# Layer 1's gate products moved from the third query chunk to the attention's last units

## The chip, the cores and the metric

One Trainium2 chip, one core of it. The metric is the device time of one execution in microseconds (us); of several executions the median is given. A core has five engines with a queue each: PE (matrix products and transposes), DVE (vector), ACT (activations, copies), POOL (general), and SP, which here only issues transfers (DMA). Each takes its instructions in the order in which they stand; an instruction whose operand is not ready holds up everything behind it on the same engine.

## The reference

The kernel computes one inference step of a trunk with two layers on 128 context tokens and 512 latent tokens, width 1024. Layer 0 is gated grouped-query attention (16 query heads, 4 key/value heads of width 64), layer 1 a gated linear recurrence in two directions. Both are modulated by vectors that come from a conditioning vector `c` (latent tokens) or `c_ctx` (context tokens):

```
def _adaln(cond, w, b):
    mod = jax.nn.silu(cond) @ w + b
    return jnp.split(mod, 3, axis=-1)          # shift, scale, gate

for i in range(2):
    sh_p, sc_p, g_p = _adaln(c_ctx, ada_w[i], ada_b[i])
    sh_s, sc_s, g_s = _adaln(c, ada_w[i], ada_b[i])
    hp = xp * (1.0 + sc_p) + sh_p
    hs = xs * (1.0 + sc_s) + sh_s
    out_p, out_s = mixer_i(hp, hs)             # i = 0: attention, i = 1: recurrence
    xp = _layer_norm(ALPHA * xp + g_p * out_p, ln_gain[i], ln_bias[i])
    xs = _layer_norm(ALPHA * xs + g_s * out_s, ln_gain[i], ln_bias[i])
```

The gate of layer 1 (`g_p`, `g_s` with i = 1) depends only on the conditioning vectors and on a 1024 x 1024 block of `ada_w[1]`. It is used first where layer 1 closes, at the very end of the program.

## The kernel before

All tokens (five tiles of 128) stay on the core. The program runs in two halves; the first (keys, values, queries and attention of layer 0) is recorded in program order, and a scheduler that works with its own model of time then decides how the instructions of each engine follow one another. Tuned tables in the source set what the program order is.

Attention is cut in units. A unit is one query head with 256 latent tokens (`sample_unit`) or four heads with the context tokens (`prompt_unit`). A sample unit has two *fronts*, of 128 queries each: scores on PE (`sc`, lines 923 and 924), the row maximum on DVE (`nm`, line 1018), the exponential on ACT (`p`, line 1023), the reciprocal of the sum on DVE (`rc`, line 1028), and the scaling of the probabilities on POOL (line 1029). Its *back* is ten transposes on PE (`pt`, line 1036), copied out of PSUM by ACT or DVE (`pts`, line 928). Two heads together then have their products with the values on PE (`pot`, line 950), and DVE multiplies them into the gate path `gs` (line 955). Scores have two buffers in PSUM, `pot` one. Fronts run two units ahead of backs.

`att_gen` yields after every such piece, and `weave(att, side, SIDE_AT)` runs `SIDE_AT[n]` steps of side work after the n-th piece. Side work is a list that is taken from its head: the query projections of chunks 1 to 3 (`q1`, `q2`, `q3`: products `qmm`, lines 389 to 391, and their norm and rotation), then `w` (the first four pieces of the attention's output weights split into a high part by ACT, `wohi`, line 262, and a low part by DVE, `wolo`, line 264), then `s` (splits of `gs`). What is called the third query chunk is `q2`, since the first is chunk 0.

Each query chunk takes a generator as *filling* (`q_gen`, table `FILL_AT`): chunk 1 the gate products of layer 0, chunk 2 those of layer 1 (`ada_gen`), chunk 3 five column jobs (`cols_gen`: ten DVE instructions, `spill`, line 361). `ada_gen(layer)` loads the bias to `acc`, and four times takes two pieces of `ada_w` (512 KB each), multiplies them with the conditioning vectors (`ada_mms`, line 312: four products of 32 x 256 for each piece, in four column strips) and adds the sum to `acc` on DVE (line 349); at its end POOL issues four small transfers of `acc` to `gated` in DRAM (line 353). The first layer's gate is read back from there by `gate_load` (line 341) inside the last chunk's filling, the second's in the recurrence's tail.

Weights come through one ring of three 512 KB buffers (`raw`, line 241) in the order of the list `order`, issued by SP. `pump` keeps two pieces taken ahead; a piece's transfer starts when the piece three before it has been used up. So the list's order, and the engine that uses a piece, set when the next ones arrive.

Of the kernel before, what the change touches and what calls it, by code (L numbers as in the profile page):

```python
# [34 lines left out]
HALVES = ((0, 320), (320, 640))  # L35
HALF_PIECES = (slice(0, 512), slice(512, 1024))
RAW_AHEAD = 2
FILL_AT = {1: '0b0e2e', 2: '0b0e2e4e', 3: '0a0b0e2e4e'}
LEAD = (1, 1)
RAW_START = 8  # L40
EARLY = 2
# [2 lines left out]
D_OUTS = 1  # L44
SIDE_T = 2.2
SIDE_AT = (
    "0100021120010100020100012001210201010101000002111001021000000130"
    "2002020010001200011201020101300010100102000000201112120001100001"
    "3100002000111000000310010102010113001000012000120300210000012")
RES_AT = 6  # L50
SEVEN = range(1, RH - 1)
FORMS_AT = 3
# [12 lines left out]
COLS = [(s, ft) for s in range(2) for ft in range(KT)]  # L65
COLS_LATE = 5
# [88 lines left out]
def hybrid_step(ctx: ExitStack, tc: tile.TileContext, a: dict, o: dict):  # L155
# [16 lines left out]
    def bank1(name):  # L172
        if "b1" not in pools:
            return bank2(name)[:, 0, :]
        return pools["b1"].tile([P, 512], F32, tag="b1", name=name)
# [40 lines left out]
    order = deque()  # L216
    pin, pass_on = tc.keep_in_program_order, lambda ins: ins

    def pump(most=RAW_AHEAD):
        while order:  # L220
            start = order[0] in FIRST
            if len(ahead) >= (RAW_START if start else most):
                break
            src = order.popleft()
            if src[0] == "x":
                c = slice(src[1] * CW, (src[1] + 1) * CW)
                pin(nc.sync.dma_start(xt[:, :TS, c], a["xs"][:, c].rearrange("(t p) d -> p t d", p=P)))
                pin(nc.sync.dma_start(xt[:, TS, c], a["xp"][:, c]))
                continue
            if src[0] == "rope":  # L230
                rope_loads()
                continue
            if src[0] == "sil":
                for s in range(2):
                    pin(nc.sync.dma_start(silb[:, s, :], a["cond_r"][s:s + 1, :].to_broadcast((P, D))))
                continue
            raw = (raw0 if start else rawp).tile([P, 1024], F32, tag="raw", name="raw")
            if src[0] == "kvh":
                pin(nc.sync.dma_start(raw[:, :512], piece(src)))
            else:  # L240
                (pass_on if src[0][:3] == "rec" else pin)(nc.sync.dma_start(raw, piece(src)))
            ahead.append((src, raw))
# [56 lines left out]
    def take(src):  # L299
        pump()  # L300
        got, raw = ahead.popleft()
        assert got == src, (got, src)
        return raw
# [3 lines left out]
    def ada_mms(ps, sup, i):  # L307

        for k in (2 * i, 2 * i + 1):
            raw = take(("ada_s", sup, k))  # L310
            for q in range(4):
                nc.tensor.matmul(ps[32 * q:32 * q + 32, :CW], sil[:, k, :], raw[:, q * CW:(q + 1) * CW],
                                 start=(k % 2 == 0), stop=(k % 2 == 1))
            pump()
# [24 lines left out]
    def gate_load(layer, eng):  # L339
        for s in range(2):  # L340
            eng.dma_start(gate[layer][:, s, :], gated[layer][s:s + 1, :].to_broadcast((P, D)))

    def ada_gen(layer):
        acc = rowp.tile([P, CW], F32, tag="row", name="acc")
        nc.gpsimd.dma_start(acc, a["ada_bias"][layer])
        for i in range(4):
            ps = bank1("adaps")
            ada_mms(ps, layer, i)
            nc.vector.tensor_tensor(acc, acc, ps[:, :CW], ALU.add)
            yield  # L350
        yield
        for q in range(4):
            nc.gpsimd.dma_start(gated[layer][:, q * CW:(q + 1) * CW], acc[32 * q:32 * q + 2, :])
        yield

    def ada_cols(job, raw, spill, after):

        s, ft = job
        for c in range(2):
            with tc.issue_after(after()) if after else ExitStack():  # L360
                nc.vector.scalar_tensor_tensor(spill(), raw, 1.0, silb[:, c, :], ALU.mult, ALU.mult,
                                               accum_out=shsc[1][:, s, ft, c:c + 1])
            yield
        if ft == KT - 1:
            nc.vector.tensor_tensor(shsc[1][:, s], shsc[1][:, s], view(adab, (3 + s) * KT, [[1, KT], [0, 2]]), ALU.add)
# [4 lines left out]
    def cols_gen():  # L370
        for job in COLS[len(COLS) - COLS_LATE:]:
            yield from ada_cols(job, take(("ada_c",) + job), spare, None)
            pump()
        gate[0] = gsp.tile([P, 2, D], F32, tag="gate", name="gate0")
        gate_load(0, nc.gpsimd)
# [29 lines left out]
    def pieces(name, c, n=2):  # L405
        return [(name, c, i) for i in range(n)]

    PIECES = [(nh, i) for nh in range(2) for i in range(4)]
    OUT1 = [(nh, i) for i in range(4) for nh in range(2)]
    def ada_pieces(sup):  # L410
        return [("ada_s", sup, k) for k in range(KT)]
# [16 lines left out]
        order.extend(pieces("attn_w_in", c))  # L428
    for c in range(3):
        order.extend(pieces("attn_w_in", c + 1))  # L430
        order.extend(ada_pieces(c) if c < 2 else [("ada_c",) + job for job in COLS[len(COLS) - COLS_LATE:]])
    order.extend(("attn_w_out", nh, i) for nh, i in PIECES)
    order.extend(("rec_w_in", h, i) for h in range(RH) for i in range(5))
    order.extend(("rec_w_out", nh, i) for nh, i in OUT1)

# [200 lines left out]
    def rms_stat(ps, n):  # L636
        ss = tiny.tile([P, 8], F32, tag="ss", name="ss")
        squares(ps, n, ss[:, :4 * n])
        rstd = tiny.tile([P, 8], F32, tag="rstd", name="rstd")
        rsqrt(rstd[:, :4 * n], ss[:, :4 * n], 1.0 / HD, NORM_EPS)  # L640
        return rstd
# [29 lines left out]
    def rms_scale(r, n, rstd):  # L671
        qn = prep.tile([P, 2 * CW], F32, tag="qn", name="qn")
        nc.vector.tensor_tensor(view(qn, 0, [[HD, 4 * n], [1, HD]]), view(r, 0, [[HD, 4 * n], [1, HD]]),
                                view(rstd, 0, [[1, 4 * n], [0, HD]]), ALU.mult)
        return qn
# [63 lines left out]
    def tok_unit(w, tt0, n, name):  # L739
        ps = bank1(name)  # L740
        for i in range(n):
            yield from tok_gen(ps[:, i * CW:(i + 1) * CW], w, tt0 + i, hhi, hlo)
        return ps

    def q_gen(c, X, fill):

        w = Weights("attn_w_in", c, (nc.vector, nc.vector), tuple(last_split))
        yield
        spots = {FILL_AT[c][i:i + 2] for i in range(0, len(FILL_AT[c]), 2)}
        pend = None  # L750
        for tt0, n in UNITS:
            ps = None
            gen = tok_unit(w, tt0, n, "qmm")
            step = 0
            while ps is None:
                try:
                    next(gen)
                except StopIteration as e:
                    ps = e.value
                    break  # L760
                step += 1
                yield
                if f"{tt0}{'0abcd'[step]}" in spots:
                    next(fill, None)
                    yield
            rstd = rms_stat(ps, n)
            r = rope_raw(ps, tt0, n, cosq, sinq, qg)
            yield
            if pend:
                for i in range(pend[1]):  # L770
                    pend[0](i)
                    yield
            if f"{tt0}e" in spots:
                next(fill, None)
                yield
            yield
            qn = rms_scale(r, n, rstd)
            yield
            pend = (q_split(qn, tt0, n, c % 2, X, bank1), n)
        yield  # L780
        for _ in fill:
            yield
        for i in range(pend[1]):
            pend[0](i)
            yield

    xq = [rpool("xq0", 1)]
    Xs = {0: xq[0].tile([P, 4, NT], F32R, tag="X", name="X0")}
# [218 lines left out]
    back_of = [0]  # L1007
# [97 lines left out]
    side = Side()  # L1105
# [57 lines left out]
    def split_gs(ks):  # L1163
        for k in ks:
            split_act(hhi[:, k, :], hlo[:, k, :], gs[:, k, :], nc.gpsimd if k < 6 else nc.vector)
            yield
# [4 lines left out]
    def prefetch_gen():  # L1171
        wb.close()
        pq.close()
        woa.append(ws.enter_context(pool("woa", 1)))
        yield from wo_gen(0, PIECES[:4], woa[0])

    def q_next(c):
        Xs[c] = xq[c % 2].tile([P, 4, NT], F32R, tag="X", name=f"X{c}")
        yield from q_gen(c, Xs[c], ada_gen(c - 1) if c < 3 else cols_gen())

    for c in range(1, 4):
        side.items.append((f"q{c}", q_next(c), lambda c=c: front_of[0] >= c - 1))
    side.items += [("w", prefetch_gen()), ("s", split_gs(range(6)), lambda: back_of[0] == 3)]
    for _ in range(3):
        side.step()
    with tc.issue_after(last_qmm[0]):
# [705 lines left out]
    side = token_forms()  # L1892
    for h in range(RH):
        H = {} if h else H
        if h == RH - 1:
            sxs.close()
            side = reload_gen()
# [203 lines left out]
```

## Time and profile before

| | us |
|---|---|
| median of 3 runs | 820.88 |
| lowest, highest | 820.34, 822.41 |
| the profiled execution, its time | 820.92 |
| its span | 819.2 |

The span is the time from the first to the last instruction that the profiler recorded; 1.7 us of the time lie around it. In the profile PE is a busy matrix engine, PEld its weight loads. A row of a view by stretches gives start:end, the length, and for PE, PEld, DVE, ACT and POOL the busy time with the number of instructions; the last three are the granted clock of PE, the DMA engines' busy share, and GB/s. In the profiled execution the query chunks and the attention's units lie at 134 to 325 us; the products of layer 1's gate at 193 to 229 us; the last product of the last query chunk at 269.1 us; the column jobs at 234 to 288 us; the first four output-weight splits at 291 to 301 us; the first product of the output projection at 325.0 us.

### The profile page before, as it was taken

What the parts mean: (1) busy time and instruction counts of PE and PEld (TensorE: products, weight loads), DVE (VectorE), ACT (ScalarE), POOL (GpSimd) and SP (SyncE); (2) the same over time, 40 slices, a digit from 0 to 9 for tenths busy, and PEclk for the clock granted to TensorE, in tenths of its full rate; (3) what the DMA queues carried; (4) which work ended last, traced back from release to release, by engine and by line L of the source; (5) the groups of instructions that cost most, each with busy time, mean ns of one, the idle gap of its engine ahead of it and who ended that gap; (6) DMA issues with size and microseconds to landing.
All of it is one profiled execution on the core that took longest, in us unless ns stands there. A gap on an engine that the chain in (4) does not pass through costs nothing.

```text
span 819.2 us, 19274 instructions
## 1 busy us (share of the span) xinstructions
PE 792.4 (97%) x7953; PEld 700.9 (86%) x7953; DVE 598.3 (73%) x1083; ACT 447.0 (55%) x890; POOL 215.1 (26%) x261
## 2 busy tenths in 40 slices
PE   8999999999999989999999999999999999999994
PEld 6789999878888766888899999998999999897874
DVE  4567767686678885676799787868787876788376
ACT  2252545566566786132565666757484855766242
POOL 0124001353434843011500224122240404131121
PEclk9999999999999999999999999999999999999998
DMA  9944344234130150621431342324242344232341
GB/s 327 395 158 157 104 155 134 100 110 150 52 129 28 36 197 18 240 103 50 141 104 54 100 118 76 104 69 125 64 134 72 103 102 162 70 110 74 136 153 77
DMA packets 36630, 98.12 MB, mean 120 GB/s; under 512 B 5296, under 2 KB 12480, under 8 KB 36544
## 3 DMA queue, kind: packets, MB, share of 16 engines
q1 hardware_dynamic: 25872, 78.95, 28.7%
q0 software_dynamic: 4768, 14.18, 5.8%
q10 hardware_dynamic: 5904, 3.78, 1.6%
q8 instruction: 62, 1.02, 0.5%
q14 instruction: 24, 0.20, 0.1%
HBM read 86.06 MB, written 10.83 MB: 118 GB/s over the span
## 4 chain that ended last, share of the span: by engine, by line
PE 80%; DVE 8%; DMA 4%; ACT 3%; issue 2%; POOL 2%; SPq 0%; DVEq 0%; ACTq 0%; POOLq 0%
PE vgps L1383 8%; PE vgps L1379 4%; PE outp L1213 4%; PE outp L1215 4%; PE outp L1214 4%; PE rps L1451 4%; PE pot L950 3%; PE rps L1405 3%; PE rps L1407 3%; PE rps L1406 3%; PE pt L1036 3%; PE rps L1453 3%; PE rps L1452 3%; PE acc L568 3%; PE lv L1682 2%
## 5 line engine op out<-in xcount | busy, mean ns | idle before, releaser
L1029 POOL TENSOR_SCALAR p<-p,rc 128x640 f32<-128x640 f32 x64 | 56.9, 894 | 115.5 <-DVE rc L1028 98.3
L1720 POOL COPY At<-near 32x160 f32<-32x160 f32 x32 | 15.0, 469 | 191.8 <-PE lv L1688 173.7
L1023 ACT ACTIVATE p<-sc,nm 128x640 f32<-128x640 f32 x64 | 51.1, 801 | 25.2 <-DVE nm L1018 15.5
L1018 DVE TENSOR_REDUCE nm<-sc 128x1 f32<-128x640 f32 x64 | 51.7, 816 | 12.7 <-PE sc L924 12.6
L1405 PE MATMUL rps<-h1hi,rw 128*128 128x320 f32 x176 | 55.4, 315 | 0.0
L1407 PE MATMUL rps<-h1hi,rw 128*128 128x320 f32 x176 | 54.5, 310 | 0.1
L1406 PE MATMUL rps<-h1lo,rw 128*128 128x320 f32 x176 | 54.5, 309 | 0.0
L1036 PE MATMUL pt<-small,p 128*128 128x128 f32 x320 | 49.0, 277 | 3.0 <-DVE pts L928 1.2
L1383 PE MATMUL vgps<-rw,h1hi 128*128 128x512 f32 x180 | 48.3, 392 | 0.0
L1655 ACT COPY kc<-A 128x640 f32<-128x640 f32 x47 | 37.5, 798 | 18.5 <-DVE A L1706 12.5
L1036 PEld LDWEIGHTS pt<-small,p 128*128 128x128 f32 x320 | 36.5, 140 | 12.0 <-issue 5.6
L928 ACT COPY pts<-pt 128x512 f32<-128x512 f32 x64 | 36.1, 589 | 14.8 <-PE pt L1036 14.6
L923 PE MATMUL sc<-kk,X 128*128 128x320 f32 x128 | 42.4, 340 | 1.8 <-ACT p L1023 1.6
L1726 ACT COPY At<-lv 32x160 f32<-32x160 f32 (+1 forms) x48 | 15.8, 329 | 49.6 <-PE lv L1688 49.2
L950 PE MATMUL pot<-pts,vv 128*64 128x256 f32 x320 | 38.3, 384 | 2.1 <-DVE pts L928 2.0
L380 PE MATMUL gps<-hhi,whi 128*128 128x320 f32 x128 | 40.0, 312 | 0.1
L381 PE MATMUL gps<-hlo,whi 128*128 128x320 f32 x128 | 39.6, 309 | 0.0
L382 PE MATMUL gps<-hhi,wlo 128*128 128x320 f32 x128 | 39.5, 309 | 0.0
L1383 PEld LDWEIGHTS vgps<-rw,h1hi 128*128 128x128 f32 x180 | 33.1, 188 | 6.6
L924 PE MATMUL sc<-klo,X 128*128 128x320 f32 x128 | 38.6, 310 | 0.0
L1383 PE MATMUL vgps<-wspare,h1hi 128*128 128x512 f32 x140 | 38.1, 394 | 0.0
L389 PE MATMUL qmm<-whi,hhi 128*128 128x256 f32 x120 | 35.0, 292 | 0.1
(347 smaller groups left out, 2623.2 us busy)
## 6 DMA issues: line engine op xcount, KB each, us to landing
raw<-in_rec_w_in SPq DMA_DIRECT2D x40, 512.0 KB, 3.8
raw<-in_ada_m SPq DMA_DIRECT2D x16, 512.0 KB, 8.3
raw<-in_attn_w_in SPq DMA_DIRECT2D x16, 512.0 KB, 4.6
raw<-in_ada_s SPq DMA_DIRECT2D x16, 512.0 KB, 3.7
adaraw<-in_ada_c SPq DMA_DIRECT2D x11, 512.0 KB, 5.4
raw<-in_attn_w_out SPq DMA_DIRECT2D x8, 512.0 KB, 4.1
raw<-in_rec_w_out SPq DMA_DIRECT2D x8, 512.0 KB, 3.6
raw<-in_ada_c SPq DMA_DIRECT2D x5, 512.0 KB, 4.4
```

The source lines that it names most:

```text
L380: nc.tensor.matmul(ps[:, :320], w.hi(k)[:, c], hhi[:, k, t], start=(k == 0), stop=False)
L381: nc.tensor.matmul(ps[:, :320], w.hi(k)[:, c], hlo[:, k, t], start=False, stop=False)
L923: nc.tensor.matmul(out, X[:, h, t0:t0 + P], kk[:, c, k0:k1], start=True, stop=False)
L950: nc.tensor.matmul(pot[j * HD:(j + 1) * HD, :CW], vv[:, slot, c * HD:(c + 1) * HD], moving[j], start=first, stop=last)
L1018: nc.vector.tensor_reduce(nm[:, 0:1], sc[:, :, :320], AX.XY, ALU.max, negate=True)
L1023: return nc.scalar.activation(halves(p[:]), sc[:, :, :320], AF.Exp, bias=nm[:, 0:1], accum_out=su[:, 0:1])
L1029: nc.gpsimd.tensor_scalar(p, p, rs[:, 0:1], 1.0, ALU.mult, ALU.mult)
L1036: nc.tensor.transpose(pt[:, i * 256 + q * P:i * 256 + (q + 1) * P], ps[q][:, (k0 + i) * P:(k0 + i + 1) * P], ident)
L1383: nc.tensor.matmul(out, h1hi[:, k, t], wvg[i][:, k % 4].rearrange("p e n -> p (e n)"), start=(k == 0), stop=(k == KT - 1))
L1405: nc.tensor.matmul(ps[:, j, :320], hi[:, k, :], h1hi[:, k, t], start=(k == 0), stop=False)
L1406: nc.tensor.matmul(ps[:, j, :320], hi[:, k, :], h1lo[:, k, t], start=False, stop=False)
L1407: nc.tensor.matmul(ps[:, j, :320], lo[:, k, :], h1hi[:, k, t], start=False, stop=(k == KT - 1))
```

## The change

The gate products of layer 1 leave the filling of chunk 2 (its entry in `FILL_AT` is empty, and its generator too) and become an item of their own, `g`, in the side list, behind `w` and ahead of `s`. In the order of weight pieces their eight pieces move from behind chunk 2's weights to a place behind the first four pieces of the output weights. `SIDE_AT` loses the steps that the filling took and has its last third laid out anew.

```diff
-FILL_AT = {1: '0b0e2e', 2: '0b0e2e4e', 3: '0a0b0e2e4e'}
+FILL_AT = {1: '0b0e2e', 2: '', 3: '0a0b0e2e4e'}
 SIDE_AT = (
-    "0100021120010100020100012001210201010101000002111001021000000130"
-    "2002020010001200011201020101300010100102000000201112120001100001"
-    "3100002000111000000310010102010113001000012000120300210000012")
+    "0100021120010100020100012001210201010101000001110001021000000130"
+    "1002020010001100011101020101300010100102000000201112120001100001"
+    "3100002000100001001001001201111010100000000000000000000000000")
...
         order.extend(pieces("attn_w_in", c + 1))
-        order.extend(ada_pieces(c) if c < 2 else [("ada_c",) + job for job in COLS[len(COLS) - COLS_LATE:]])
-    order.extend(("attn_w_out", nh, i) for nh, i in PIECES)
+        order.extend(((lambda: ada_pieces(0)), list, lambda: [("ada_c",) + job for job in COLS[len(COLS) - COLS_LATE:]])[c]())
+    order.extend(("attn_w_out", nh, i) for nh, i in PIECES[:4])
+    order.extend(ada_pieces(1))
+    order.extend(("attn_w_out", nh, i) for nh, i in PIECES[4:])
...
-        yield from q_gen(c, Xs[c], ada_gen(c - 1) if c < 3 else cols_gen())
+        yield from q_gen(c, Xs[c], (ada_gen(0), iter(()), cols_gen())[c - 1])
...
-    side.items += [("w", prefetch_gen()), ("s", split_gs(range(6)), lambda: back_of[0] == 3)]
+    side.items += [("w", prefetch_gen()), ("g", ada_gen(1)), ("s", split_gs(range(6)), lambda: back_of[0] == 3)]
```

What the scheduler makes of it differs in many small places between the second query chunk and the attention's end; no instruction is added or taken away. Lines behind the edits are two higher in the changed kernel (312, 349 and 353 stay; `sc` is 925 and 926, `pt` 1038, `pot` 952).

SP's queue, before: the transfers of weight pieces from chunk 2's weights on (`ada_s` are gate pieces, `ada_c` the column jobs').

```order
L241 DMA raw<-in_attn_w_in 128x1024 x2
L241 DMA raw<-in_ada_s 128x1024 x8
L241 DMA raw<-in_attn_w_in 128x1024 x2
L241 DMA raw<-in_ada_c 128x1024 x5
L241 DMA raw<-in_attn_w_out 128x1024 x8
```

And in the changed kernel, the same place:

```order
L241 DMA raw<-in_attn_w_in 128x1024 x4
L241 DMA raw<-in_ada_c 128x1024 x5
L241 DMA raw<-in_attn_w_out 128x1024 x4
L241 DMA raw<-in_ada_s 128x1024 x8
L241 DMA raw<-in_attn_w_out 128x1024 x4
```

The eight gate pieces moved past chunk 3's weights, the column jobs and four output pieces; the last four output pieces come behind them.

PE's queue, before: where the last two pieces' products of a gate step stood, among scores and transposes of the second chunk's units, ahead of chunk 3's projection.

```order
L924 MATMUL sc<-klo,X_1580 128x320
L734 MATMUL qps<-identr,qs_2473 128x128 x4
L312 MATMUL adaps<-raw,sil 32x256 x8
L1036 MATMUL pt<-small,p 128x128 x6
L923 MATMUL sc<-kk,X_1580 128x320
```

In the changed kernel the first five pieces' products stand here, behind a product with the values (`pscp` are the scores of the last context unit; the rows of its four heads, and of the second half of a front, are alike and left out):

```order
L952 MATMUL pot<-pts,vv 64x256 x10
L312 MATMUL adaps<-raw,sil 32x256 x4
L1038 MATMUL pt<-small,p 128x128 x4
L312 MATMUL adaps<-raw,sil 32x256 x4
L1038 MATMUL pt<-small,p 128x128 x4
L925 MATMUL sc<-kk,X_2863 128x320
...
L926 MATMUL pscp<-klo,X_2863 128x128
L312 MATMUL adaps<-raw,sil 32x256 x4
L1038 MATMUL pt<-small,p 128x128 x2
L312 MATMUL adaps<-raw,sil 32x256 x8
L1038 MATMUL pt<-small,p 128x128 x4
```

All 32 products of layer 1's gate moved from the second chunk's units to the last units, and stand close together there.

DVE's queue in the changed kernel, at the fourth and last of the early output-weight splits:

```order
L264 TENSOR_TENSOR wolo<-raw,wohi 128x1024
L1020 TENSOR_REDUCE nm<-sc 128x1
L1030 RECIPROCAL rc<-su 128x1 x2
L957 TENSOR_TENSOR gs<-pot,gs 128x256
L349 TENSOR_TENSOR acc<-acc,adaps 128x256
L1020 TENSOR_REDUCE nm<-sc 128x1
L978 TENSOR_REDUCE nmp<-pscp 128x4
```

The first addition to `acc` moved behind the fourth split, ahead of two row maxima.

## The prediction

> **What bounds the kernel now.** I read the page's shares and its chain first, then the stretches of the attention, then what PE waited for there, then the chain in order of time.
>
> ```profile
> PE 792.4 (97%) x7953; PEld 700.9 (86%) x7953; DVE 598.3 (73%) x1083; ACT 447.0 (55%) x890; POOL 215.1 (26%) x261
> PE 80%; DVE 8%; DMA 4%; ACT 3%; issue 2%; POOL 2%; SPq 0%; DVEq 0%; ACTq 0%; POOLq 0%
> ```
>
> PE is busy for 792.4 of 819.2 us. The change neither adds nor removes work, so it can move the end only through the 26.8 us in which PE stands still. Where are they? The rows by stretches (columns as the document gives them: first the busy time of PE, third that of DVE, fifth that of POOL):
>
> ```profile
> 186.00:232.00 46.00, 45.94 (x403) 38.50 (x402) 30.32 (x69) 28.60 (x66) 18.98 (x22) 1.00 0.30 96
> 232.00:269.00 37.00, 36.18 (x296) 32.13 (x296) 28.64 (x60) 23.07 (x54) 14.73 (x16) 1.00 0.19 68
> 269.00:301.00 32.00, 27.27 (x207) 21.11 (x206) 28.14 (x56) 24.57 (x50) 23.68 (x21) 1.00 0.39 132
> 301.00:316.00 15.00, 14.80 (x115) 11.09 (x113) 9.58 (x23) 11.59 (x31) 7.34 (x8) 1.00 0.11 37
> 316.00:325.00 9.00, 7.63 (x63) 5.11 (x61) 3.83 (x10) 5.04 (x11) 2.39 (x3) 1.00 0.01 2
> ```
>
> In the second chunk's stretch (186 to 232, where the gate products are) PE loses 0.1 us, so whatever leaves it shortens it. Of the 7 us that PE loses from 232 on, 4.7 lie between 269 and 301, behind the last query product, where DVE is busy for 28.1 of 32. From 301 to 316 PE is full again (14.80 of 15), and 1.4 are lost at the very end. The granted clock is 1.00 throughout. What held PE from 232 to 326:
>
> ```profile
> PE pot L950 <- DVE pts L928: 2.0, 2, 1.5
> PE sc L923 <- ACT p L1023: 1.4, 3, 0.7
> PE pt L1036 <- DVE pts L928: 1.2, 2, 1.0
> PE pt L1036 <- POOL p L1029: 0.9, 2, 0.7
> PE pt L1036 <- ACT pts L928: 0.9, 2, 0.5
> ```
>
> These are parts of the softmax pipeline, all of them behind DVE or fed by it. The chain in order of time (start, us, engine) tells what DVE was late with:
>
> ```profile
> 286.85 1.73 DVE spill L361 x3
> ...
> 291.21 0.64 DVE wolo L264
> ...
> 292.45 6.07 DMA raw<-in_attn_w_out
> 298.54 1.05 ACT wohi L262
> 299.62 0.81 DVE wolo L264
> ```
>
> So between 279 and 301 the path is not PE at all: it runs through five column jobs on DVE, the first output-weight split, the transfer that this split's buffer lets start (6.07 us), and the fourth split. Behind that PE works off what has piled up, and from 301 to the end the path is PE's again, except for the last two waits.
>
> **The change part by part.** First, what leaves the second chunk. The gate products there, and what one step of them takes (a step of layer 0, of the same shape, with the instruction that follows it):
>
> ```profile
> 186.00:232.00 46.00, 4.49 (x64) 1.56 (x64) 1.67 (x4) 1.00 0.30 96
> ...
> 178.72 1.07 PE L312 MATMUL adaps<-raw,sil 128*32 128x256 f32 x16
> 179.82 2.38 PE L950 MATMUL pot<-pts,vv 128*64 128x256 f32 x20
> ```
>
> From 178.72 to 179.82 is 1.10 us for a step, 4.4 for the four (4.49 busy). PE is full there, so 4.4 us go: **-4.4**. That is also what it would cost if nothing covered it: all that can be won is 4.4, and what waits shrink besides. The other engines lose four additions (1.7 us of DVE) and POOL four issues, neither on the path there.
>
> Second, where the products arrive. By PE's order they begin behind a value product which itself needs DVE's copies and the previous value product's result taken away (one `pot` buffer), and that stands on DVE behind the third split. Their data come later still: the first three gate pieces go into the buffers that the second, third and fourth output splits free. None of them can therefore fill the idle time before the splits are done; they fall where PE was full in 301 to 316: **+4.4**, cover none.
>
> Third, how long the DVE-bound part lasts. From the last query product to the fourth split it took 269.2 to 300.8. The changed order has the same five column jobs and four splits in it; ten row maxima became twelve, and six copies of transposes four, and the group's rows price them:
>
> ```profile
> L361 DVE SCALAR_TENSOR_TENSOR spill<-raw,silb 128x1024 f32<-128x1024 f32 x5 | 7.2, 1456 | 0.0
> L1018 DVE TENSOR_REDUCE nm<-sc 128x1 f32<-128x640 f32 x8 | 6.5, 809 | 0.2 <-PE sc L924 0.2
> L264 DVE TENSOR_TENSOR wolo<-raw,wohi 128x1024 fp32r<-128x1024 f32 x4 | 5.0, 1259 | 1.1 <-ACT wohi L262 1.1
> L928 DVE COPY pts<-pt 128x256 f32<-128x256 f32 x5 | 2.0, 408 | 0.0
> ```
>
> Two times 0.81 less two times 0.41 is 0.8 more. But a value product now follows the last query product at once, where two fronts' scores stood between (2 x 0.67 by the rows below): 1.3 less. The part becomes 0.5 shorter, 31.5 for 32.0 (counted from 269). What can PE do in it? By the order, before the first gate product it has 24 transposes fewer than before in the same part, no scores of the context unit, and one front's scores more. Prices, by start to next start:
>
> ```profile
> 313.70 1.23 PE pt L1036 x10
> ...
> 277.34 0.39 PE L923 MATMUL sc<-kk,X 128*128 128x320 f32 x1
> 278.01 0.27 PE L1036 MATMUL pt<-small,p 128*128 128x128 f32 x1
> ...
> 296.78 0.33 PE L923 MATMUL pscp<-kk,X 128*128 128x128 f32 x1
> 297.82 2.38 PE L950 MATMUL pot<-pts,vv 128*64 128x256 f32 x20
> ```
>
> 24 x 0.123 = 3.0 less, 1.0 less, 0.7 more: 27.3 - 3.3 = 24.0 us of work. The first piece's products and the four transposes behind them (half a step, 0.55, and 0.5) may still be done: 25.0. PE stands still for 31.5 - 25.0 = 6.5 instead of 4.7, and the work that it has not done then comes in the full part. The count says +1.8. DVE was idle there for 32.0 - 28.1 = 3.9 us too; if the order takes that away, the term is 1.8 - 3.9 = -2.1, and if it adds as much again as the count does, it is +3.6. I take **+1.4**, a tenth of the way from the count to the lower end, since the count rests on the order of PE and DVE and the lower end on nothing that I saw.
>
> Fourth, the new waits. PE now stands at the second piece's product until that piece has landed, and behind PE's wait stand transposes and scores; DVE's first addition waits for PE, and behind it stand two row maxima, which ACT's exponentials wait for. The ring has three buffers, and the transfers' times to landing are
>
> ```profile
> raw<-in_ada_s SPq DMA_DIRECT2D x8, 512.0 KB, 3.6
> raw<-in_attn_w_out SPq DMA_DIRECT2D x5, 512.0 KB, 4.0
> gate<-gated POOLq DMA_DIRECT2D x2, 512.0 KB, 7.4
> ```
>
> (the first from 180 to 232, the others from 285 to 300). The third and the fourth split on DVE were
>
> ```profile
> 295.65 1.39 DVE L264 TENSOR_TENSOR wolo<-raw,wohi 128x1024 fp32r<-128x1024 f32 x1
> ...
> 299.62 1.22 DVE L264 TENSOR_TENSOR wolo<-raw,wohi 128x1024 fp32r<-128x1024 f32 x1 [1.06 <-ACT wohi L262]
> ```
>
> The second gate piece starts when the third split ends (297.0), 3.8 us ahead of the fourth's end (300.8): it lands at about the fourth's end. The third starts with the fourth's end, and PE is there after half a step, four transposes, a front and the context scores, 0.55 + 0.5 + 0.7 + 1.0 = 2.8 us later: 0.8 us too early. The fourth to eighth start when a product frees a buffer, and by the same prices PE comes to them 0 to 0.2 early. Sum 1.0 by these, nothing if the second chunk's 3.6 holds and PE is a little late. I take **+0.5**; the upper end is in the second rival.
>
> [...]
>
> Fifth, the end. The last waits were these (in brackets the idle time and who ended it):
>
> ```profile
> 320.28 1.28 PE L1036 MATMUL pt<-small,p 128*128 128x128 f32 x10 [0.33 <-ACT pts L928]
> 322.08 2.38 PE L950 MATMUL pot<-pts,vv 128*64 128x256 f32 x20 [0.52 <-DVE pts L928]
> 324.98 0.50 PE L1213 MATMUL outp<-wohi,hhi 128*128 128x512 f32 x1 [0.53 <-DVE gs L955]
> ```
>
> In the new order a value product of 2.3 us stands between the last two groups of transposes and covers the first two waits in part: **-0.5** (0 to -0.85). DVE's four additions and POOL's four issues to `gated`
>
> ```profile
> L349 DVE TENSOR_TENSOR acc<-acc,adaps 128x256 f32<-128x256 f32 x4 | 1.7, 417 | 0.3 <-PE adaps L312 0.3
> 230.18 2.11 POOL L353 DMA_DIRECT2D gated<-acc  x4
> ```
>
> go where DVE has 13.4 of 24 us to do (the two last rows by stretches) and POOL 9.7: nothing. If that cover were gone, they would cost 1.7 and 2.1. The earlier weights of the last chunk, the earlier column pieces and the later output pieces (used from 325 on, ordered some 15 us ahead) cost nothing while PE is full.
>
> Sum: -4.4 + 4.4 + 1.4 + 0.5 - 0.5 = +1.4. The profiled execution took 820.92 (span 819.2 and 1.7 around it), the median 820.88, the same within 0.1. **822.3 us.**
>
> **The rivals.** *Slower: the ring of three buffers sets the pace of the last units.* The chain's 6.07 us is a transfer of the same size in the same place, with the read of the first gate (7.4 to land) beside it. If the gate pieces take that long, PE waits 6.1 - 3.8 = 2.3 at the second piece, 6.1 - 2.3 - 2.8 = 1.0 at the third, and at the other pieces, by then with less beside them, some 1.0 more: 4.3 instead of 0.5, 826.1. It decides from about 5 us to landing on. For it: the chain's row. Against: it is one transfer, and the median in that window is 4.0.
>
> *Faster: the path through DVE gets shorter.* The column jobs took 1456 ns each from 279 to 301, but in the stretch before that
>
> ```profile
> L361 DVE SCALAR_TENSOR_TENSOR spill<-raw,silb 128x1024 f32<-128x1024 f32 x5 | 6.0, 1219 | 1.2 <-DMA raw<-in_ada_c 1.2
> ```
>
> If the new order draws them apart from POOL's splits, 5 x 0.24 = 1.2 go; if the transfer behind the first split takes 3.6 for 6.07, 2.5 go; with that the new waits (0.5) go too: 822.3 - 4.2 = 818.1. For it: the changed DVE order spreads the column jobs over one row maximum more. Against: their number, and the splits', is the same, and the read of the first gate still falls beside the transfer. [...]
>
> *Nothing comes of it:* the removed 4.4 and the added 4.4 cancel and PE's idle time is unchanged: 820.9. It lies inside the forecast's own range and counts with it.
>
> **How the numbers follow.** This measurement can tell about 0.3% from no change, 2.5 us: below 818.4 is faster, above 823.3 slower. The forecast has 0.58, with a range of its own of 820.3 to 824.0; of that 0.45 lie within 0.3%, 0.12 above, 0.01 below. The faster rival has 0.22 (0.21 below 818.4, 0.01 within), the slower one 0.20 (all above). Together: faster 0.22, same 0.46, slower 0.32. The range must reach to both rivals' times: 817.8 to 825.6, which leaves out about 0.2.
>
> **What would show it.** In the changed profile: (1) PE's stretch of the second chunk 4.4 us shorter, and the last query product at about 264 us (4.4 less, and 1.3 for two fronts' scores that now come behind it); a later one falls on the first term. (2) PE's idle time from there to the fourth split some 6 us, behind DVE; if it is under 4, the third term was wrong. (3) Waits of PE at line 312 for `raw<-in_ada_s`, and of DVE at line 349 for PE, of 0.5 us together; several us mean the slower rival. (4) PE full from the fourth split on for some 30 us, with the gate products in it. (5) The first product of the output projection at about 326.4. The forecast is wrong altogether if gate products run inside the DVE-bound part, for then the second term has cover after all.

## The result and the profile after

The changed kernel takes 832.84 us (median of 6 runs, 831.13 to 834.45), beside 821.25 for the kernel before on the same chip: 1.014 times as long, with an interval of 1.0121 to 1.016. That is about 11.5 us slower. I had forecast 822.3, with a range up to 825.6.

Where the 10 us between the two profiled executions lie (spans 819.2 and 829.2) is told by three rows of each timeline: the first and the last query product, and the first output product. Before:

```profile
134.79 0.28 PE L389 MATMUL qmm<-whi,hhi 128*128 128x256 f32 x1
269.10 0.28 PE L391 MATMUL qmm<-whi,hlo 128*128 128x256 f32 x1
324.98 0.50 PE L1213 MATMUL outp<-wohi,hhi 128*128 128x512 f32 x1 [0.53 <-DVE gs L955]
```

After:

```profile
134.08 0.28 PE L389 MATMUL qmm<-whi,hhi 128*128 128x256 f32 x1
266.61 0.28 PE L391 MATMUL qmm<-whi,hlo 128*128 128x256 f32 x1
335.97 0.50 PE L1215 MATMUL outp<-wohi,hhi 128*128 128x512 f32 x1 [0.53 <-DVE gs L957]
```

I call the stretch between the first two rows "the chunks" and the one between the last two "the rest". The chunks went from 134.31 to 132.53 (-1.8), the rest from 55.88 to 69.36 (+13.5). Lengths are compared and not places, because the first query product falls between 133.5 and 138.3 us in the executions below, though nothing ahead of it was edited. The remaining -1.7 lie ahead of the first row and behind the third.

The stretches of the changed kernel (PE's busy time first, the granted clock third from the right), cut at the last query product and at the fourth output-weight split's end:

```profile
186.00:232.00 46.00, 43.72 (x350) 38.22 (x350) 32.14 (x65) 28.37 (x65) 16.87 (x17) 1.00 0.12 41
232.00:266.75 34.75, 33.55 (x272) 29.34 (x270) 23.28 (x51) 19.48 (x46) 14.80 (x15) 1.00 0.07 23
266.75:299.35 32.60, 26.11 (x168) 18.68 (x168) 28.91 (x57) 23.57 (x48) 20.65 (x20) 0.90 0.40 129
299.35:335.97 36.62, 33.17 (x287) 22.38 (x283) 18.26 (x42) 20.20 (x48) 13.47 (x17) 1.00 0.39 131
```

and the last two of them in the kernel before:

```profile
269.20:300.84 31.64, 26.91 (x204) 20.75 (x203) 27.98 (x56) 24.21 (x50) 23.48 (x20) 1.00 0.40 133
300.84:324.98 24.14, 22.58 (x176) 16.33 (x174) 13.57 (x33) 16.76 (x42) 9.73 (x11) 1.00 0.07 23
```

Three things are new. In 186 to 232 PE, which had stood still for 0.1 us, now stands still for 2.3. Over the whole of the chunks its busy time fell by 4.4 (132.72 to 128.37) and its idle time grew by 2.6 (1.59 to 4.16). In the third row the clock is 0.90. And the last part is 36.62 long where it had been 24.14, with PE busy in 33.17 of it for 22.58.

What PE waited for in the second and third chunk (total, times, longest), where the kernel before has one wait of 0.7:

```profile
PE sc L925 <- ACT p L1025: 2.0, 3, 0.7
PE pt L1038 <- POOL p L1031: 0.6, 1, 0.6
PE qmm L389 <- DVE pts L930: 0.5, 1, 0.5
```

The scores wait for the exponentials of earlier scores to free one of two banks, the transposes for a scaled tile, the query products for a copy: the softmax pipeline, which the gate products had been hiding.

The clock fell at 292.28, behind two waits of the same kind and ahead of a third. The timeline of PE, and windows around the fall:

```profile
290.46 0.41 PE L925 MATMUL sc<-kk,X 128*128 128x320 f32 x1 [1.59 <-ACT p L1025]
291.72 0.42 PE L925 MATMUL sc<-kk,X 128*128 128x320 f32 x1 [0.41 <-ACT p L1025]
294.38 0.63 PE L925 MATMUL sc<-kk,X 128*128 128x320 f32 x1 [1.67 <-ACT p L1025]
296.81 3.49 PE L952 MATMUL pot<-pts,vv 128*64 128x256 f32 x20
```

```profile
288.86:292.28 3.42, 1.42 (x9) 1.15 (x8) 3.42 (x6) 3.42 (x8) 0.84 (x2) 1.00 0.87 241
292.28:295.70 3.42, 1.75 (x8) 1.35 (x7) 3.42 (x9) 2.00 (x5) 1.60 (x2) 0.50 0.85 307
295.70:299.12 3.42, 3.42 (x17) 2.14 (x17) 1.98 (x5) 1.83 (x3) 1.58 (x2) 0.50 0.81 303
299.12:302.54 3.42, 3.42 (x37) 1.82 (x34) 1.93 (x6) 1.73 (x4) 1.64 (x3) 1.00 0.56 169
```

For 6.8 us PE ran at half its clock: the value product, most of which lies in that time, took 3.49 us for the 2.38 it takes elsewhere. PE was busy for 1.75 + 3.42 = 5.17 us of that, which is 2.6 us of work at full clock done in 5.2: an estimate of 2.6 lost. The rows above are laid from the fall, each half of its 6.8 us long: the one ahead of it was busy for 1.42 of 3.42 us, and the longest gap in it was 1.59.

The chain of waits in order of time, where the pieces enter it:

```profile
300.30 0.61 PE adaps L312 x8
300.92 0.02 issue
300.93 4.69 DMA raw<-in_ada_s
305.62 0.04 issue
305.67 0.68 PE adaps L312 x8
306.35 0.02 issue
306.37 4.52 DMA raw<-in_ada_s
310.89 0.14 issue
311.02 0.64 PE adaps L312 x8
```

A product frees a buffer, a transfer of 4.69 us goes into it, and the product three pieces on waits for that. Over the stretch PE waited so:

```profile
PE adaps L312 <- DMA raw<-in_ada_s: 2.0, 3, 0.7
```

### The profile page after: what moved, and what is told of

The parts are those of the page before. It is cut to its first block, busy times and chain, and to the rows that moved or that the text cites. A ratio compares the mean times of both kernels' runs of the same rounds, so it can differ in the third digit from the quotient of the medians.

```text
span 829.2 us, 19281 instructions
## 1 busy us (share of the span) xinstructions
PE 796.6 (96%) x7953; PEld 700.5 (84%) x7953; DVE 601.3 (73%) x1083; ACT 447.4 (54%) x890; POOL 214.9 (26%) x261
## 4 chain that ended last, share of the span: by engine, by line
PE 78%; DVE 10%; DMA 4%; ACT 3%; issue 3%; POOL 1%; SPq 0%; DVEq 0%; ACTq 0%; POOLq 0%
PE vgps L1385 8%; PE vgps L1381 4%; PE pot L952 4%; PE outp L1215 4%; PE outp L1217 4%; PE outp L1216 4%; PE rps L1453 3%; PE rps L1407 3%; PE rps L1409 3%; PE rps L1408 3%; PE rps L1455 3%; PE rps L1454 3%; PE pt L1038 3%; PE lv L1684 2%; PE sc L925 2%
```

## The experiments

Theory A, from this reading: in the second chunk the products had lain in gaps, so little is won there; behind it the loss is of four kinds, the products' own time, a clock that falls, waits for pieces, and the new order. The rivals: the ring of three buffers is the whole loss; or it is the transfers' share of the memory; or the order alone. The program's scheduler arranges the instructions by its own reckoning of when data arrive, so nearly every edit also moves something; where PE's order stayed equal I say so. All ratios and lengths together, with the time at half clock within the chunks and the rest (lengths and times in us):

| run | ratio to the kernel before | chunks | rest | half clock |
|---|---|---|---|---|
| kernel before | 1 | 134.31 | 55.88 | 0 |
| changed kernel | 1.014 (1.0121 to 1.016) | 132.53 | 69.36 | 6.8 |
| changed kernel again | not compared | 132.51 | 69.44 | 6.8 |
| no products | 1.0009 (0.9995 to 1.0022) | 132.77 | 59.43 | 3.4 |
| half moved | 1.0103 (1.0088 to 1.0118) | 133.48 | 64.16 | 6.8 |
| double at the old place | 1.0179 (1.0154 to 1.0204) | 139.99 | 63.27 | 6.8 |
| space of their own | 1.0105 (1.0079 to 1.0131) | 132.54 | 66.03 | 3.4 |
| the same, earlier | 1.0148 (1.0121 to 1.0175) | 132.51 | 67.91 | 0 |
| filler | 1.0121 (1.0094 to 1.0148) | 132.50 | 68.57 | 0 |
| data there | 1.0074 (1.0059 to 1.0089) | 132.52 | 61.40 | 0 |
| pieces unread | 1.0061 (1.0037 to 1.0085) | 132.49 | 61.81 | 0 |
| fourth buffer | 1.0114 (1.008 to 1.0147) | 132.52 | 67.61 | 6.8 |
| filler and fourth buffer | 1.011 (1.0074 to 1.0147) | 132.54 | 67.13 | 0 |

**No products.**

```diff
-            ps = bank1("adaps")
-            ada_mms(ps, layer, i)
-            nc.vector.tensor_tensor(acc, acc, ps[:, :CW], ALU.add)
+            if layer == 0:
+                ps = bank1("adaps")
+                ada_mms(ps, layer, i)
+                nc.vector.tensor_tensor(acc, acc, ps[:, :CW], ALU.add)
...
-    order.extend(ada_pieces(1))
```

> The changed kernel without layer 1's gate products, their additions and their pieces (so its second gate is only the bias). Taking the same out of the kernel before gives the same order on every engine, so this one run prices the products at both places. The prediction's sum: without them the second chunk gives 4.4 back, the DVE-bound part loses 1.4: 820.9 - 4.4 + 1.4 - 0.5 = 817.4, so they are worth 3.5 at the old place and 15 at the new one. Theory A (in the second chunk the products had covered softmax waits, and the rest of the loss is in the order that follows): 2 of the 4.4 only, and the four fronts of scores in a row with the halved clock remain: 832.8 - 4.4 (products) - 3 (waits for pieces) = 825, slower than the kernel before. The PE clock in 285 to 305 us tells whether the drop needs the products at all.

It took 821.43, the kernel before's time: the products cost next to nothing where they were, and 11 us where they are now. So no move of them alone could have won much: even if every execution lost the 1.7 us to the clock that the profiled one did (below), 819.7 would be left, 1.1 less than the 820.85 of the kernel before beside it. The prediction's 817.4 is out by 4, and theory A's 825 by nearly as much on the other side, since it carried over the changed kernel's losses. In the chunks PE's waits are those of the changed kernel to the digit (2.0, 0.6 and 0.5).

The rest grew by 3.55 with no product in it. Two fronts' scores that stood ahead of the last query product stand behind it (88 score products there instead of 80): 8 x 0.15 = 1.2. And the clock fell here too, for one window and at another place:

```profile
278.31:281.73 3.42, 1.84 (x15) 1.55 (x14) 3.42 (x10) 1.89 (x5) 1.07 (x1) 1.00 0.44 135
281.73:285.15 3.42, 3.42 (x15) 2.86 (x17) 3.42 (x9) 2.39 (x5) 0.80 (x1) 0.50 0.12 31
```

PE was busy for all of that window, so half of it is lost: 1.7 by estimate. Together 2.9 of the 3.55. This fall may owe something to chance: the half moved run passed an emptier window, of 1.71, without a fall (see the last section). With the fronts counted, taking out 4.4 us of products and pushing 1.2 us of scores behind shortened the chunks by 1.5, so it brought 0.3 in all.

**Half moved.** Two steps stay in the second chunk.

```diff
-FILL_AT = {1: '0b0e2e', 2: '', 3: '0a0b0e2e4e'}
+FILL_AT = {1: '0b0e2e', 2: '0b0e', 3: '0a0b0e2e4e'}
...
+    gate1 = ada_gen(1)
...
-        yield from q_gen(c, Xs[c], (ada_gen(0), iter(()), cols_gen())[c - 1])
+        yield from q_gen(c, Xs[c], (ada_gen(0), islice(gate1, 2), cols_gen())[c - 1])
```

> Two of the four steps stay in the second chunk, two are moved, with their four pieces. By the runs so far the two that stay are free, and the two moved cost half of 11.4: 826.5. If the loss is in the waits of the later pieces (three buffers hold the first three): 2.2 for the work and about 1 for one wait, 824. If the clock's drop comes with any gap: 2 more.

828.0, or 8.0 us more than the kernel before by the medians and 8.4 by the ratio: above the 824 to 826.5 expected and more than half of 11.5, though PE never waited for a piece. Its waits from the last query product on are of the other kind,

```profile
PE sc L926 <- ACT p L1026: 5.1, 3, 2.6
```

and the clock fell for the same 6.8 us as with all four steps moved. So the clock's price doesn't go by the number of steps, and this run is no half of the loss.

**Double at the old place.** The kernel before, with a second set of products in the second chunk.

```diff
+            for q in [0, 1, 2, 3] * 2 if sup and k % 2 else []:
+                nc.tensor.matmul(ps[32 * q:32 * q + 32, CW:2 * CW], sil[:, k, :], raw[:, q * CW:(q + 1) * CW],
+                                 start=True, stop=True)
```

> The kernel before, with each step of layer 1's products in the second chunk followed by eight more products of the same shape that nobody reads (into unused columns of its bank): 4.4 us more PE work at the old place. Without any products the time was 821.4, with one set 820.9. Cover theory: PE's gaps behind the softmax hold one set and no more (0.1 us was left of them), so the second set costs in full: 820.9 + 4.4 = 825.3. If the second chunk is bound by another engine throughout and PE merely looks full: under 822.5.

835.65, ten more than the 825.3 of the cover theory. The chunks' lengths by the amount of products in the second one are now a curve: none 132.5 to 132.8, half a set 133.5, one set 134.3, two sets 140.0. The first set costs 1.8 of its 4.4, the second 5.7. But the kernel before has two fronts' scores (1.2) more in its chunks than all other runs, this one included; with them counted the first set costs 0.3 to 0.6 and the second 6.9. The kernel before stands at the knee, which fits the cover theory. That the second set costs more than its own time, and that the rest grew as well (the fronts and 3.1 for the clock explain 4.3 of its 7.4), it does not explain: PE's idle time in the chunks grew by 2.1 (1.59 to 3.65), and the cause was not looked for further.

**Filler to hold the clock.** Into unused columns of the score banks:

```diff
+            fronts_done[0] += 1
+            for _ in range({51: 2, 52: 2, 53: 4}.get(fronts_done[0], 0)):
+                for n in range(2):
+                    score_mms(sc[:, n, 320:512], Xs[c], c, h, (2 * qh + i) * P, 0, 192)
```

> The changed kernel with extra products that nobody reads: after the fronts 51, 52 and 53 (counted over the sample units) 2, 2 and 4 times four products of 192 columns into unused columns of the score bank, 2.9 us of PE work in all, where it stood still before its clock fell. Clock theory: the granted clock stays at 1.00 from 290 to 300, 5.5 us of work no longer take twice the time: -2.7, with 0 to 1 for what of the filler isn't covered: 830 to 831. If the clock's drop costs nothing beside the waits: 832.8 to 834.

The clock stayed at 1.00 from the first query product to the first output product. The window in which PE had been busy for 1.42 of 3.42 us, and the next one, are these here (the same two counted from the last query product, within 0.2 us):

```profile
289.36:292.77 3.41, 2.40 (x19) 1.99 (x17) 3.41 (x9) 3.41 (x7) 1.52 (x3) 1.00 0.87 274
292.77:296.19 3.42, 2.87 (x23) 2.88 (x24) 2.42 (x6) 1.38 (x4) 1.78 (x3) 1.00 0.89 316
```

The time fell by 1.6 us (1.0121 for 1.014), although 2.9 us of work were added. The intervals overlap, so a gain in time is not shown. That filling the gaps kept the clock up is shown, by this run and the later one with the same order on PE.

**The changed kernel again**, for whether the fall is chance.

> The changed kernel once more, for where its clock falls. If the fall comes from the gaps that the order sets, the granted clock is 0.50 from about 292 to 299 again; if it is chance, it is elsewhere or 1.00.

The clock fell behind the same waits, for the same 6.8 us (295.84 to 302.7), in an execution whose last query product lies 3.6 us later:

```profile
292.42:295.84 3.42, 1.42 (x8) 1.09 (x8) 3.42 (x6) 3.42 (x8) 0.90 (x2) 1.00 0.80 246
295.84:299.26 3.42, 1.80 (x8) 1.40 (x7) 3.42 (x8) 2.07 (x5) 1.60 (x2) 0.50 0.87 247
```

So the fall repeats with the same order. But it came 25.6 us behind the last query product, as the first did with 25.7, so the two executions test one position of the windows in time and not several.

**Pieces in space of their own**, all loaded ahead of the output weights, and **the same with the products drawn earlier**:

```diff
+    def own_load():
+        spaces = [hp.tile([P, KT, NT], F32, tag=t, name="own" + t) for t in ("hhi", "hlo")]
+        for n in range(KT):
+            raw = spaces[n // 4][:, n % 4 * 2:n % 4 * 2 + 2, :].rearrange("p a b -> p (a b)")[:, :1024]
+            pin(nc.sync.dma_start(raw, piece(("ada_s", 1, n))))
+            own.append(raw)
...
         woa.append(ws.enter_context(pool("woa", 1)))
+        own_load()
```

> The eight pieces in space of their own (that of the query operand, free after the last query product), all loaded at once ahead of the output weights; the products at the same place of the table. Ring theory (second rival): no wait at line 312 for a piece, and the output weights' own transfers shorter: 832.8 - 3 to 4 = 829. If the three buffers cost nothing: 832 to 833.

> As the run with space of their own, and the products drawn from between the output-weight splits on, in the stretch bound by DVE. Cover theory: 3 to 4 of the 4.4 us of products fall into PE's idle time there, PE's clock stays at 1.00 because it is busier, DVE's path gets 4 additions of 0.42: 829 - 3.5 - 2.7 + 1.7 = 824.5. If cover there is worth nothing (the path is DVE's and the products only shift it): 829 or more.

The first took 829.15, as the ring theory had it, but that is no support: its output-weight splits came far later, and its products ran ahead of them. The second, 833.67, missed its 824.5. SP's queue shows why in both (these rows are the first's, up to 312 us; start, and how long the queue was held by the group):

```profile
275.33 5.48 SPq L241 DMA_DIRECT2D raw<-in_attn_w_out  x2
280.85 1.92 SPq L312 DMA_DIRECT2D ownhhi<-in_ada_s  x4
282.81 2.24 SPq L312 DMA_DIRECT2D ownhlo<-in_ada_s  x4
285.44 25.36 SPq L241 DMA_DIRECT2D raw<-in_attn_w_out  x5
```

The eight pieces stood in the queue behind an output piece that waited for its buffer, and the later output pieces stood behind them: the third and fourth split came at 305.6 and 309.0 instead of 294.1 and 298.1, and in the second run at 306.5 and 309.2. I had counted buffers and forgotten the queue.

**Data there, and pieces unread.** The products read a tile that lies on the chip; in the second run the pieces are still loaded through the ring.

```diff
-                nc.tensor.matmul(ps[32 * q:32 * q + 32, :CW], sil[:, k, :], raw[:, q * CW:(q + 1) * CW],
+                nc.tensor.matmul(ps[32 * q:32 * q + 32, :CW], sil[:, k, :],
+                                 cosq[:].rearrange("p a b -> p (a b)") if sup else raw[:, q * CW:(q + 1) * CW],
```

> The changed kernel without the eight pieces: the products at the new place read a tile that lies on the chip from the start (so the second gate is wrong). Ring theory: with no piece to wait for the products can run inside the stretch bound by DVE and cover PE's idle time there, the clock stays up: 821.4 (no products) + 4.5 - 3.5 covered + 1.7 (four additions on DVE's path) = 824. If the place itself costs, with the data there: 821.4 + 4.5 = 826 or more. If neither wait nor transfer matter: 832.

> As the run whose products read a tile that is there (ratio to the kernel before 1.0074; same order on PE), but the eight pieces are loaded through the three buffers as in the changed kernel, and nobody reads them. If the pieces cost by PE's waiting for them: 1.0074 again, 826.5. If they cost by standing in the queue, the buffers and the memory's bandwidth beside the output weights: up to the changed kernel's 1.014, 832; half way 829.

The first took 825.43 and the second 825.58. PE's order is the same in both. It differs from the changed kernel's: with data at hand the scheduler sets two of the four steps, and the beginning of the third, into the stretch that DVE bounds. The first with the data there, whose fourth split ended at 300.3:

```profile
290.44 1.07 PE L312 MATMUL adaps<-cosq,sil 128*32 128x256 f32 x16 [0.79 <-ACT pts L931]
293.74 1.07 PE L312 MATMUL adaps<-cosq,sil 128*32 128x256 f32 x16 [0.40 <-DVE acc L351]
299.58 1.07 PE L312 MATMUL adaps<-cosq,sil 128*32 128x256 f32 x16
303.04 1.07 PE L312 MATMUL adaps<-cosq,sil 128*32 128x256 f32 x16
```

The rest is 61.40 with the data there: 55.88 + 1.2 (fronts) + 4.4 (products) = 61.5. That the sum fits so well is in part chance: PE's idle time in the rest is 1.0 less than before (5.28 for 6.30), and the scores took 1.0 longer than their number says. Beside the run without products, less the 1.7 that its clock lost (59.43 - 1.7 = 57.7), the products cost 3.7. So 3.7 to 4.4 of their 4.4 us is paid, although half of them run inside the stretch where PE has gaps, with the clock at 1.00. Loading the pieces beside it adds 0.4 to the rest (61.81) and nothing to the time. The memory's share is therefore no large cause; the 7.5 us from 61.81 to 69.36 come from products that need the pieces, by their waits, by the clock, and by the order that follows from late data.

**A fourth buffer**, alone and with the filler (the orders on PE are those of the changed kernel up to the fifth piece, and of the filler run throughout):

```diff
+            fourth = src[0] == "ada_s" and src[1] == 1 and src[2] % 4 == 3
-            raw = (raw0 if start else rawp).tile([P, 1024], F32, tag="raw", name="raw")
+            raw = (raw0 if start else extra[0] if fourth else rawp).tile([P, 1024], F32, tag="raw", name="raw")
```

> The changed kernel with a fourth buffer for pieces: every fourth gate piece of layer 1 has a buffer of its own (the additions' rows have one buffer for two to make room). PE's order is the changed kernel's up to the fourth product step. Ring theory: the later pieces start one piece earlier, the 2.0 us of waits at line 312 and most of the small gaps around them go: 832.8 - 2 to 3 = 830 (ratio to the kernel before 1.0105 to 1.012 for 1.014). If the rate of the transfers (half a MB in 4.6 us) sets the pace and not the number of buffers: 832 to 833.

> Filler that held the clock (ratio 1.0121) and the fourth buffer together; the order on PE is the filler run's, word for word. If ring and clock are two costs that add: 1.0121 less 2 to 3 us, 1.009 (828.3). If the fourth buffer does nothing: 1.012.

Alone it shortens the rest by 1.75 (67.61), beside the filler by 1.44 (67.13 from 68.57). PE's wait for pieces in the latter, where the filler alone has 2.3 in 3:

```profile
PE adaps L314 <- DMA raw<-in_ada_s: 0.6, 2, 0.4
```

So by the lengths, of one execution each, the ring is worth about 1.5 to 2 us, and it and the filler add up only in part: 2.2 for both together (67.13 from 69.36). Both together took 1.011 of the kernel before's time, between the 1.009 and the 1.012 expected. By the time alone neither run can be told from the changed kernel (1.008 to 1.0147 and 1.0074 to 1.0147 against 1.0121 to 1.016).

## Why the prediction was wrong

**First term (what leaves the second chunk, -4.4): this step failed first.** It said that PE is full there, so 4.4 us go. PE was full, and yet the chunks became only 1.8 shorter, and 1.2 of these are scores that moved behind, so 0.6 is left of the 4.4. Busy for all but 0.1 us does not mean that nothing else was about to bind: scores, transposes and query products that wait for ACT, POOL and DVE stood just behind the gate products, and 3.1 us of their waits stand there where one of 0.7 had been. The run without products shows the same waits and nearly the same length (132.77 for 132.53). Point (1) of the list of what would show it, a last query product at 264, had 266.6 and fell on this term, as it said. The count that the prediction did not make is which softmax results would be late if PE came 4.4 us earlier.

**Second term (+4.4, no cover): right in the main.** In the changed kernel no product runs ahead of the fourth split. The run with the data there has 4.3 after the fronts, or 3.7 beside the run without products. The sentence that the second term has cover if products run inside the DVE-bound part was mostly wrong: half of them run there, and at most 0.7 of their 4.4 is covered.

**Third term (the part that DVE bounds, +1.4): wrong by a cost that it did not have.** The part's length was to be 31.5 and was 32.6; PE's idle time in it was to be 6.5 and was 6.5 (32.60 - 26.11). But of the 26.11 busy some 2.6 are half-clock time, so PE had 3.4 us less done than before by its end (26.91 - 23.5), not the 2.3 of the count. With the length, 1.0 + 3.4 = 4.4 instead of 1.4; 2.6 of the missing 3.0 are the clock. The prediction read the granted clock as 1.00 and took it for a constant, while its own third term added idle time to PE: here windows of 3.4 us with 1.4 us of PE's work brought the fall, and with 2.4 in the same place it stayed away. The faster rival counted 1.2 us for column jobs drawn apart from POOL's splits. In the kernel before the five jobs ahead of the last query product, with no POOL instruction beside them, took 1.21 to 1.23 us each; of the five behind it, all with one beside them, three took 1.51 (beside a split), 1.60 and 1.73 (beside the scaling of probabilities), and two 1.21 and 1.23. That POOL is the cause no run tested.

**Fourth term (waits on the ring, +0.5): mechanism right, size wrong.** PE waited 2.0 at line 312, and the fourth buffer gave 1.75 back. Landing took 4.6 in the median and not the 3.6 of the second chunk or the 4.0 of the earlier output pieces; eight pieces now go after each other without a pause (DMA share 0.82 from 301 to 316, where it had been 0.11). These waits were the slower rival's, at 826.1; it had the right sign and some 2 of the 11.5. The range was meant to reach to both rivals' times and ended at 825.6, short of it; the measured time lies beyond both.

**Fifth term (the end, -0.5): -0.2.** Three waits are left there, 0.5 for a copy, 0.5 for the last result and 0.2 for a score bank, for the 1.4 before.

The rest's 13.5 by these: fronts 1.2, products 4.4, clock 2.6, waits for pieces 2.0, which is 10.2. Of the other 3.3, PE's idle time explains 1.7 (9.94 against 6.29 before, less the 2.0 for pieces): scores that wait for banks, since up to four fronts follow each other without other work between. The last 1.6 are PE's own busy time. Counted once, for the product that began first and without the half-clock share, the 88 score products took 15.2 us where 80 took 12.9, which is 1.1 more than their number says; the gate products took 4.8 for 4.4 and the transposes 0.5 more, and smaller differences take 0.3 off. The groups are cut smaller: four transposes in a row took 0.65 us, ten 1.23 to 1.28. That this cutting is the reason was not tested. In the profiled executions, 10.0 apart where 1.4 was forecast, the miss of 8.6 is then 3.8 in the first term (-0.6 for -4.4), 3.0 in the third, 1.5 in the fourth, 0.3 in the fifth and 1.7 for the longer products, less the 1.7 outside the chunks and the rest.

Of the five signs, the second came true (6.5 us of PE's idle time), on a part that was slow for another reason. The third had 2.0 us of waits for pieces and 1.9 of DVE for PE at line 349 where it had 0.5 together. The fourth did not come true: from the fourth split on PE stood still for 3.45 of 36.62 us. The fifth, a first output product at 326.4, had 336.0.

## What to carry to other kernels

An engine that is busy for all of a stretch isn't thereby its only bound: before counting work that leaves it as won, look for what waits directly behind, or take the work out and measure. Here one run without the products, which is the same program on every engine whichever of the two kernels they are taken from, would have shown that no place for them could win more than about 1 us. And an edit that opens gaps in PE's work can have a second price, its clock: in these runs the busy share of every 3.4 us told more than the single gaps. In the kernel before a gap of 1.52 us, in a window with 1.89 us of work, left the clock at 1.00; in the changed kernel one of 1.59, in a window with 1.42, stood ahead of the fall to 0.50.

## What was not expected of the hardware

Between the first query product and the first output product the clock fell to 0.50 for 3.4 or 6.8 us and nothing between, in seven of the thirteen executions profiled, after windows of 3.4 us in which PE had been busy for 1.2 to 2.1 us and had no gap as long as the window. A similar busy share didn't always bring it: the kernel before has a stretch of 3.4 us with 1.7 busy at 1.00.

In these traces that went with where the stretch lies. In twelve executions the records hold more than one half-clock stretch (the one behind the last products counts too), and all their starts are whole multiples of 3.413 us apart, up to 239 of them (235 in the kernel before, from 9.34 to 811.47 us, and 155 in the changed kernel, from 292.28 to 821.35). That gives each execution its own row of windows, and the stretch of the kernel before is not one of them: it lies across two. Of the windows at full clock in these rows, between the same two products, all five in which PE was busy for 1.70 us or less were followed by a fall. Of the seven with 1.71 to 2.10 two were (1.83 and 2.10), and none of the 746 others was. The half moved run has two nearly equal windows side by side, of 1.71 and 1.63, the first without a fall (the next window is at full clock) and the second with one:

```profile
288.30:291.71 3.41, 1.71 (x12) 1.35 (x12) 3.41 (x9) 3.41 (x7) 3.38 (x4) 1.00 0.58 184
291.71:295.13 3.42, 1.63 (x8) 1.18 (x8) 3.42 (x9) 2.59 (x6) 0.71 (x2) 1.00 0.89 259
```

The emptiest of the kernel before holds 1.89. The rows lie at different places against the program in different executions (the fall of the run without products came 15.0 us behind its last query product, that of the fourth buffer 24.4). In the changed kernel's trace every position of the row would have put a window of at most 1.84 us there; in the kernel before's the emptiest window would hold 1.7 to 2.3. No run set the position, so what decides between 1.7 and 2.1 stays open.
